# Three large and two small PSUM tiles, and softmax probabilities transposed as fp32r from a copy, in a gated encoder layer

## The chip, the cores and the metric

One NeuronCore of a Trainium2 chip runs the whole kernel. The metric is device time in microseconds (us) of one execution, as the median of repeated runs; three runs of the kernel before gave 1495.1, 1495.29 and 1495.49 us, so the time is repeatable to well under 0.1%. Beside the timed runs stands one execution under the hardware profiler, from which all durations below come.

Engines: PE is TensorE (matmul; PEld is its weight load), DVE is VectorE, ACT is ScalarE, POOL is GpSimd, SP is SyncE, which here issues the transfers.

## The reference

One layer of an encoder, applied to two groups of requests with the same weights: "prompt" with 1024 tokens and "sample" with 512, both with 1024 channels and 256 memory tokens, all in fp32.

```python
h = rms_norm(x, ln_pre)
z = h @ w_in                      # 1024 -> 6400, split into the parts below
(pool_in, pool_gate, q, k, v, attn_gate, xq, x_gate, merge_logits) = split(z)
pool_out  = multiscale_pool(pool_in, w_pool, pool_scale)        # windows 2, 4, 8, 16
q, k      = rope(rms_norm(q)), rope(rms_norm(k))                # 8 query heads, 2 key heads, 64 wide
attn_out  = softmax(q k^T / 8) v                                # over all tokens of the group
cross_out = softmax(xq mk^T / sqrt(128)) mv                     # 4 heads, 256 memory tokens
branches  = pool_out * silu(pool_gate), attn_out * silu(attn_gate), cross_out * silu(x_gate)
merged    = sum_n sigmoid(merge_logits[n] + b_merge[n]) * (branches[n] @ w_branch[n])
y         = x + rms_norm(merged @ w_out, ln_post)
```

## The kernel before, in words

**Arithmetic.** fp32 accuracy comes from fp32r matmuls in threes: each operand is split into a high part (an ACT copy into an fp32r tile, line 165) and a low part (a DVE subtraction, line 162), and `mm3` (line 132) adds high x high, high x low and low x high. Line 126 is every matmul, line 130 every transpose, so groups are told apart by their tiles. A transpose is a matmul against an identity matrix: `ident` in fp32 or `identr` in fp32r. Softmax probabilities are held in fp32 `u` tiles and transposed against `ident` into an `A` tile, from which the two parts are split.

**PSUM.** There are eight banks of 512 fp32 per partition. `A()` (line 91) is a tile of two banks, used for scores and transposes; `B()` (line 94) is a tile of one bank, used for all products. Before the change there are two A and four B tiles. SBUF tiles come from fixed sets as well: seven `u` (1024 wide), fourteen `med` (2048), eight `hu` (512).

**Stages.** The order of the work is the order of the generators at the end of the kernel (lines 1089 to 1115); a list scheduler puts the instructions of each engine in a fixed order from there, with priorities (`AHEAD`, `EVAC`, `PMAX`, `PTURN`), and each engine runs its own list strictly in order.

1. Set-up: memory keys and values (`mem_phase`), and the normalised activations of the prompt group in block form (`long_h`). The row sums of squares are spread over partitions by a matmul (`spread`, line 209) and, in `long_h`, read from the B tile by the scaling.
2. Projections of the prompt group: `products` (line 318) does pairs of weight tiles by a seven-product block scheme in place of eight. Per pair the products go to the PSUM tiles X, Y, X, Z, X, Z, X, each product being 12 matmuls of 512 columns; X keeps accumulating and is copied out in between. Behind each product `background` runs a step of the tails (rotary positions, transposes of queries and keys, pooling), which also take A and B tiles. There are 25 pairs.
3. Projections of the sample group, `plain` (line 393): 24 matmuls into one B tile for each weight tile. The first part is run alone; the second part, 32 products, is the fill of stage 4.
4. The stream: 64 units of prompt self-attention (one head, 128 queries, 1024 keys), 8 of prompt cross-attention, 16 of sample self-attention, 4 of sample cross-attention. `stream` (line 888) runs for each step i the load of unit i + 2, the scores and softmax of unit i, the transposes (`turn`) of unit i - `LAG`, and the values of unit i - `LAG` - `VLAG`. `LAG` and `VLAG` are 2. `weave` (line 108) puts fill between these parts: each part gives the fill a credit of a third of 0.66 times the unit's planned cost (2560 or 3410 ns).
5. The three gated branches of the first prompt block, run after the stream (`branches`, `merge`), then its output projection, then the other prompt block and the sample block.

**Softmax of a unit.** The scores lie in an A tile; DVE takes the maximum (line 782), ACT the exponential with its sum (line 784), DVE the reciprocal (line 785), POOL scales the probabilities (line 786). `turn` transposes the eight 128x128 pieces into another A tile, and split makes the two parts.

**Queues.** All transfers are issued on SP, in its own fixed order. Finished outputs of attention (line 886) and cross-attention (line 958) are written where they are computed, so that a write that waits for POOL or DVE holds back the loads behind it.

Of the kernel before, what the change touches and what calls it, by code (L numbers as in the profile page):

```python
# [18 lines left out]
P = 128  # L19
# [42 lines left out]
def encoder_kernel(ctx: ExitStack, tc, wt, xs, xts, mt, cols, rows, rope, edge, ys):  # L62
# [169 lines left out]
    def long_h(xt, h):  # L232

        h += [[None] * 4 for _ in range(7)]
        xv = xt.rearrange("p (k t) -> p k t", k=KC)
        q = [[M(F32) for _ in range(2)] for _ in range(2)]
        for j in range(2):
            for i in range(2):
                load(q[i][j][:].rearrange("p (c n) -> p c n", c=4), xv[:, i * 4:i * 4 + 4, j * BLK:(j + 1) * BLK])
        yield  # L240
        r, sp, sq = S(16), [], []
        for j in range(2):
            sq.append([squares(q[i][j][:]) for i in range(2)])
            yield
        for j in range(2):
            rj = r[:, j * TT:(j + 1) * TT]
            mean_squares(sq[j], rj)
            rstd_of(rj)
            yield
            sp.append(spread(rj))  # L250
            yield
        b11, b12, b21, b22 = [[q[i][j][:, :D], q[i][j][:, D:]] for i in range(2) for j in range(2)]

        def scaled(i, j):
            for c in range(4):
                x = q[i][j][:, c * BLK:(c + 1) * BLK]
                v.scalar_tensor_tensor(x, x, colt[:, i * 4 + c:i * 4 + c + 1], sp[j], op0=ALU.mult, op1=ALU.mult)
# [24 lines left out]
        put(4, t3)  # L282
        put(5, b22)
        difference(t4, b21, b11)
        put(6, t4)
# [32 lines left out]
    def products(pairs, h, n, background):  # L318
# [32 lines left out]
        for p, (_, _, take) in enumerate(pairs):  # L351
# [11 lines left out]
            for i, bank in enumerate("XYXZXZX"):  # L363
                ready(p * 4 + i // 2 + LOOK)
                start = bank not in banks
                if start:
                    banks[bank] = B()
                b = banks[bank][:, :n]
                w = ops.pop((p, i))
                for c in range(4):  # L370
                    s = slice(c * P, (c + 1) * P)
# [18 lines left out]
                next(background, None)  # L390
                yield

    def plain(pairs, h, background):

        for k0, k1, take in pairs:
            for i, key in enumerate((k0, k1)):
                w, b = weights(*key), B()
# [7 lines left out]
                yield  # L405

    def summed(b, s, out=None):

# [339 lines left out]
    def from_scratch(field, bs, dt=F32):  # L748
# [3 lines left out]
            load(t[:, c * BLK:(c + 1) * BLK], field[c][:, bs])  # L752
        return t

    def attention(b, sc, kt, vt):

        bs = slice(b * BLK, (b + 1) * BLK)
# [31 lines left out]
        def turn(i):  # L789
            jp, hd, j = units[i]  # L790
            p = state.pop(i)
            if j == 0:
                state["pt", i // 2] = M()[:], M()[:]
            pv = [t.rearrange("p (c j n) -> p c j n", c=nch, j=2) for t in state["pt", i // 2]]
            tp = A()
            for c in range(nch):
                tr(tp[:, c * P:(c + 1) * P], p[:, c * P:(c + 1) * P], ident)
            tv = tp[:].rearrange("p (c n) -> p c n", c=nch)
            with tc.high_priority(PTURN):
                split(pv[0][:, :, j], pv[1][:, :, j], tv)  # L800

# [13 lines left out]
            del state["pt", i // 2]  # L815
            gated(state, jp, hd, o, gd, out, b)

        return [(ahead, scores, turn, values, i, 2560) for i in range(len(units))]

    def pairs_of(sc, kt, vt):  # L820

# [30 lines left out]
            state[i] = p  # L852

        def turn(i):
            p, tp, pt = state[i], A(), M()
            for c in range(4):
                for j in range(2):
                    tr(tp[:, c * 256 + j * P:c * 256 + (j + 1) * P], p[:, j * BLK + c * P:j * BLK + (c + 1) * P], ident)
            with tc.high_priority(PTURN):
                split(pt[:, :D], pt[:, D:], tp[:])  # L860
            state[i] = pt

        def values(i):
# [8 lines left out]
        return [(ahead, scores, turn, values, i, 2560) for i in range(len(units))]  # L872

    def gated(state, jp, hd, o, gd, out, b):
        r = slice((hd % 2) * 64, (hd % 2) * 64 + 64)
# [7 lines left out]
            v.tensor_tensor(ot[r, :256], o[0:64, :256], ot[r, :256], op=ALU.add)  # L883
        if hd % 2:
            pool.tensor_tensor(ot[:, :256], ot[:, :256], gt[:, :256], op=ALU.mult)
            nc.sync.dma_start(out[c][:, cs], ot[:, :256])

    def stream(units):

        n = len(units)  # L890
        for i in range(-2, n + LAG + VLAG):
            more = units[min(max(i, 0), n - 1)][5] * SHARE / 3
            for k, lag in enumerate((-2, 0, LAG, LAG + VLAG)):
                if 0 <= i - lag < n:
                    units[i - lag][k](units[i - lag][4])
                if k > 0 and i >= 0:
                    yield more

    def cross(b, sc, mkd, mvd):

# [36 lines left out]

        def turn(c):
            p = state[c]
            tp = A()  # L940
            for m in range(2):
                for t in range(TT):
                    tr(tp[:, m * 512 + t * P:m * 512 + (t + 1) * P], p[:, t * 256 + m * P:t * 256 + (m + 1) * P], ident)
            pt = M()
            split(pt[:, 0:1024], pt[:, 1024:2048], tp[:])
            state[c] = pt

        def values(c):
# [9 lines left out]
            nc.sync.dma_start(out[c][:, bs], g[:])  # L958

        return [(ahead, scores, turn, values, c, 3410) for c in range(NXH)]  # L960

    def branch_parts(field, bs):
        t = from_scratch(field, bs)
# [17 lines left out]
    def merge(n, gd, bs, br, acc, merged):  # L981
# [81 lines left out]
    def ending(merged, src, dst, yv, ssq, lnpost):  # L1063
# [6 lines left out]
        for t in range(TT):  # L1070
            x = U()
            load(x, src[t * P:(t + 1) * P, :])
            o = B()[:, :256]
# [39 lines left out]
    run(block(1, 0, sc, False, merged))  # L1113
    run(block(1, 1, sc, False))
    run(block(0, 0, scs, True))
# [1 line left out]

LAG, VLAG, SHARE, LOOK, WAIT = 2, 2, 0.66, 1, 6  # L1120

AHEAD, EVAC, PMAX, PTURN, LATER = 120, 200, 150, 150, 200

# [89 lines left out]
```

## Time and profile before

| what | value |
|---|---|
| median of three runs | 1495.29 us |
| profiled execution, its own time | 1496.65 us |
| its span, first to last instruction | 1494.8 us |
| mean granted TensorE clock | 0.989 |
| busy share PE / DVE / ACT / POOL | 97 / 65 / 47 / 18% |
| share of DMA engines' time | 42.7% |

The span is 1.85 us shorter than the profiled execution's time, which is 1.36 us above the median of the runs. In the prediction, rows of a timeline have start and duration in us, engine, line, operation, output <- inputs and a count; what stands in square brackets is idle time before and what ended it. Consecutive matmuls overlap (a 512-column one is shown as 0.39 us long, but the next starts 0.23 us later), so costs of PE are read from starts. Rows of groups have the busy time, the mean in ns of one, and the idle time before them with its releasers. Wait rows have the total, the number and the longest.

### The profile page before, as it was taken

What the parts mean: (1) busy time and instruction counts of PE and PEld (TensorE: products, weight loads), DVE (VectorE), ACT (ScalarE), POOL (GpSimd) and SP (SyncE); (2) the same over time, 40 slices, a digit from 0 to 9 for tenths busy, and PEclk for the clock granted to TensorE, in tenths of its full rate; (3) what the DMA queues carried; (4) which work ended last, traced back from release to release, by engine and by line L of the source; (5) the groups of instructions that cost most, each with busy time, mean ns of one, the idle gap of its engine ahead of it and who ended that gap; (6) DMA issues with size and microseconds to landing.
All of it is one profiled execution on the core that took longest, in us unless ns stands there. A gap on an engine that the chain in (4) does not pass through costs nothing.

```text
span 1494.8 us, 19564 instructions
## 1 busy us (share of the span) xinstructions
PE 1456.0 (97%) x7264; PEld 1210.1 (81%) x7264; DVE 976.5 (65%) x1215; ACT 709.6 (47%) x1083; POOL 273.3 (18%) x286
## 2 busy tenths in 40 slices
PE   7979999999999999999999999999998999999998
PEld 5768888888888888887888888888886888888887
DVE  6996586666648564747767666676775664764764
ACT  6444444544434545434656556566675233323332
POOL 1000020110000000301222222234232150250241
PEclk9989999999999999999999999999999999999999
DMA  7513233332422434344222223165446844954952
GB/s 277 172 47 106 85 114 125 108 132 66 129 92 78 158 133 128 102 150 148 64 96 80 91 68 106 58 219 173 155 155 214 286 148 132 347 193 140 336 163 84
DMA packets 88174, 211.37 MB, mean 141 GB/s; under 512 B 9872, under 2 KB 19216, under 8 KB 87312
## 3 DMA queue, kind: packets, MB, share of 16 engines
q1 hardware_dynamic: 88080, 210.14, 42.7%
q8 instruction: 57, 0.93, 0.3%
q14 instruction: 37, 0.30, 0.1%
HBM read 155.57 MB, written 54.53 MB: 141 GB/s over the span
## 4 chain that ended last, share of the span: by engine, by line
PE 85%; DMA 4%; DVE 4%; ACT 4%; issue 2%; SPq 1%; POOL 0%; DVEq 0%; POOLq 0%; ACTq 0%
PE B L126 66%; PE A L126 14%; PE A L130 5%; ACT u L784 1%; DVE s L782 1%; ACT whi L165 1%; DMA raw<-wt 1%; DVE wlo L162 1%; PE B L130 1%; DMA hu<-xq 1%; ACT med L165 1%; SPq L139 1%; DMA u<-x_prompt 0%; DMA hu<-merge 0%; DMA hu<-x_gate 0%
## 5 line engine op out<-in xcount | busy, mean ns | idle before, releaser
L126 PE MATMUL B<-med,whi 128*128 128x512 f32 x2776 | 871.2, 394 | 15.8 <-ACT med L165 15.8
L126 PEld LDWEIGHTS B<-med,whi 128*128 128x128 f32 x2776 | 515.8, 189 | 122.2 <-ACT med L165 17.5
L126 PE MATMUL B<-med,wlo 128*128 128x512 f32 x1388 | 544.1, 392 | 0.6 <-DVE wlo L162 0.6
L126 PEld LDWEIGHTS B<-med,wlo 128*128 128x128 f32 x1388 | 261.9, 189 | 56.6 <-DVE wlo L162 1.7
L162 DVE TENSOR_TENSOR wlo<-raw,whi 128x1024 fp32r<-128x1024 f32 (+1 forms) x169 | 213.3, 1263 | 141.6 <-ACT whi L165 140.7
L165 ACT ACTIVATE whi<-raw 128x1024 fp32r<-128x1024 f32 (+1 forms) x169 | 167.5, 991 | 288.5 <-PE B L126 198.3
L165 ACT ACTIVATE med<-A 128x1024 fp32r<-128x1024 f32 x92 | 94.3, 1025 | 108.4 <-PE A L130 108.2
L162 DVE TENSOR_TENSOR med<-A,med 128x1024 fp32r<-128x1024 f32 (+1 forms) x93 | 113.0, 1215 | 42.0 <-ACT med L165 40.8
L187 POOL TENSOR_SCALAR s<-s 128x16 f32<-128x16 f32 (+3 forms) x17 | 6.9, 404 | 669.0 <-DVE s L556 333.2
L786 POOL TENSOR_SCALAR u<-u,s 128x1024 f32<-128x1024 f32 x64 | 72.1, 1127 | 251.3 <-DVE s L785 219.1
L130 PE MATMUL A<-ident,u 128*128 128x128 f32 x784 | 102.8, 273 | 0.9 <-DVE med L162 0.2
L130 PEld LDWEIGHTS A<-ident,u 128*128 128x128 f32 x784 | 90.1, 140 | 16.3 <-issue 5.2
L998 POOL TENSOR_TENSOR med<-med,hu 128x512 f32<-128x512 f32 x48 | 77.0, 1617 | 142.3 <-DVE hu L996 142.2
L782 DVE TENSOR_REDUCE s<-A 128x1 f32<-128x1024 f32 x64 | 78.1, 1220 | 32.9 <-PE A L126 11.3
L126 PE MATMUL A<-kt,med 128*128 128x512 f32 x320 | 91.9, 409 | 2.7 <-ACT u L784 1.2
L126 PE MATMUL A<-whi,med 128*128 128x512 f32 (+1 forms) x320 | 92.4, 368 | 0.2 <-ACT hu L1027 0.2
L784 ACT ACTIVATE u<-A,s 128x1024 f32<-128x1024 f32 x64 | 71.3, 1114 | 38.4 <-DVE s L782 38.0
L165 ACT ACTIVATE whi<-sum 128x1024 fp32r<-128x1024 f32 x50 | 53.1, 1062 | 65.6 <-PE B L126 63.7
L162 DVE TENSOR_TENSOR med<-med,med 128x1024 fp32r<-128x1024 f32 (+1 forms) x50 | 55.8, 1127 | 38.1 <-ACT med L165 34.2
L165 ACT ACTIVATE med<-med 128x1024 fp32r<-128x1024 f32 (+1 forms) x44 | 44.2, 1017 | 74.8 <-POOL med L998 36.2
L162 DVE TENSOR_TENSOR wlo<-sum,whi 128x1024 fp32r<-128x1024 f32 x50 | 61.1, 1221 | 23.3 <-ACT whi L165 22.4
L126 PE MATMUL B<-med,vt 128*128 128x256 f32 x512 | 75.9, 287 | 0.4 <-ACT med L165 0.4
(179 smaller groups left out, 1610.4 us busy)
## 6 DMA issues: line engine op xcount, KB each, us to landing
raw<-wt SPq DMA_DIRECT2D x168, 512.0 KB, 3.7
merge<-hu SPq DMA_DIRECT2D x72, 256.0 KB, 2.0
hu<-merge SPq DMA_DIRECT2D x72, 256.0 KB, 5.2
med<-br SPq DMA_DIRECT2D x36, 256.0 KB, 5.6
q<-hu SPq DMA_DIRECT2D x24, 256.0 KB, 2.6
br<-hu SPq DMA_DIRECT2D x24, 256.0 KB, 2.3
med<-q SPq DMA_DIRECT2D x12, 512.0 KB, 5.0
med<-xt_prompt SPq DMA_DIRECT2D x4, 1024.0 KB, 13.2
```

The costliest lines, as they stand in the source:

```text
L126: pe.matmul(out, l, r, **k)
L130: pe.transpose(out, x, i[:])
L139: return nc.sync.dma_start(out, src)
L162: v.tensor_tensor(out, x, hi.bitcast(F32), op=ALU.subtract)
L165: act.activation(hi, x, AF.Copy)
L187: pool.tensor_scalar(ss, ss, EPS, 1.0, op0=ALU.add, op1=ALU.mult)
L782: v.reduce_max(mx[:], a[:], axis=AX.X, negate=True)
L784: act.activation(p, a[:], AF.Exp, bias=mx[:], accum_out=sm[:])
L786: pool.tensor_scalar(p, p, rc[:], 1.0, op0=ALU.mult, op1=ALU.mult)
L998: pool.tensor_tensor(at, at, sg[:], op=ALU.add)
```

## The change

- A tiles go from two to three, B tiles from four to two (eight banks either way).
- In `products`, X is taken from the A tiles (half of it is used); Y and Z stay B tiles. `plain` takes its tile from a function: A and B in turn when run alone, B when it is the fill. `merge` takes A and B in turn after the stream and B within it; the last output columns take both in turn.
- In `long_h` the spread sums are copied by ACT into an `hu` tile, instead of being read in PSUM.
- Probabilities of all 92 units are copied from their `u` tile into another one declared fp32r, by a DMA of 512 KB issued on ACT (`handed`), one step after their softmax; the transposes read the copy against `identr`, into an A tile declared fp32r. `LAG` goes from 2 to 3.
- The fill is the second part of the sample projections chained with the branches of the first prompt block; in the steps behind the last unit the credit of the fill is doubled.
- Writes of finished attention outputs are collected and issued at the end of the next step.

```diff
     def A(dt=F32):
-        return ps.tile([P, 1024], dt, tag="A", bufs=2, name=nm("A"))
+        return ps.tile([P, 1024], dt, tag="A", bufs=3, name=nm("A"))
     def B(dt=F32):
-        return ps.tile([P, 512], dt, tag="B", bufs=4, name=nm("B"))
+        return ps.tile([P, 512], dt, tag="B", bufs=2, name=nm("B"))
...
-            sp.append(spread(rj))
+            sp.append(HU())
+            spread(rj, sp[j][:])
...
                 if start:
-                    banks[bank] = B()
-                b = banks[bank][:, :n]
+                    banks[bank] = (A() if bank == "X" else B())[:, :n]
+                b = banks[bank]
...
+    def either(i):
+        return (A() if i % 2 else B())[:, :BLK]
...
+    def handed(p):
+        t = U(F32R)
+        act.dma_start(t.bitcast(F32), p)
+        return t
+
+    def hand_on(state):
+        def hand(i):
+            state[i] = handed(state[i])
+        return hand
...
-            tp = A()
+            tp = A(F32R)
             for c in range(nch):
-                tr(tp[:, c * P:(c + 1) * P], p[:, c * P:(c + 1) * P], ident)
+                tr(tp[:, c * P:(c + 1) * P], p[:, c * P:(c + 1) * P], identr)
...
-            nc.sync.dma_start(out[c][:, cs], ot[:, :256])
+            finished.append((out[c][:, cs], ot[:, :256]))
...
         for i in range(-2, n + LAG + VLAG):
-            more = units[min(max(i, 0), n - 1)][5] * SHARE / 3
-            for k, lag in enumerate((-2, 0, LAG, LAG + VLAG)):
+            more = units[min(max(i, 0), n - 1)][6] * SHARE / 3 * (1 + (i >= n))
+            late = finished[:]
+            finished.clear()
+            for k, lag in enumerate((-2, 0, LAG, LAG + VLAG, 1)):
                 if 0 <= i - lag < n:
-                    units[i - lag][k](units[i - lag][4])
-                if k > 0 and i >= 0:
+                    units[i - lag][k](units[i - lag][5])
+                if 0 < k < 4 and i >= 0:
                     yield more
+            for out, x in late:
+                nc.sync.dma_start(out, x)
...
-            pj = B()
+            pj = either(d) if bare else B()
...
-    run(plain(pairs[0], hs, bg))
+    run(plain(pairs[0], hs, bg, either))
     merged = []
-    fill = drained(plain(pairs[1], hs, bg))
+    fill = drained(plain(pairs[1], hs, bg, single))
...
+    bare = False
+    fill = chain(fill, branches(0, sc, merged))
     weave(stream(units), fill)
+    bare = True
     run(fill)
-    run(branches(0, sc, merged))
...
-LAG, VLAG, SHARE, LOOK, WAIT = 2, 2, 0.66, 1, 6
+LAG, VLAG, SHARE, LOOK, WAIT = 3, 2, 0.66, 1, 6
```

More of the change, by code (lines that the diff above doesn't have):

```diff
@@ L391, in products, with plain @@
                 yield
-    def plain(pairs, h, background):
+    def plain(pairs, h, background, bank):
         for k0, k1, take in pairs:
             for i, key in enumerate((k0, k1)):
-                w, b = weights(*key), B()
+                w, b = weights(*key), bank(i)
                 for k in range(KC):
@@ L816, in values @@
             gated(state, jp, hd, o, gd, out, b)
-        return [(ahead, scores, turn, values, i, 2560) for i in range(len(units))]
+        return [(ahead, scores, turn, values, hand_on(state), i, 2560) for i in range(len(units))]
     def pairs_of(sc, kt, vt):
@@ L854, in turn @@
         def turn(i):
-            p, tp, pt = state[i], A(), M()
+            p, tp, pt = state[i], A(F32R), M()
             for c in range(4):
                 for j in range(2):
-                    tr(tp[:, c * 256 + j * P:c * 256 + (j + 1) * P], p[:, j * BLK + c * P:j * BLK + (c + 1) * P], ident)
+                    tr(tp[:, c * 256 + j * P:c * 256 + (j + 1) * P], p[:, j * BLK + c * P:j * BLK + (c + 1) * P], identr)
             with tc.high_priority(PTURN):
-                split(pt[:, :D], pt[:, D:], tp[:])
+                split(pt[:, :D], pt[:, D:], tp[:].bitcast(F32))
             state[i] = pt
@@ L870, in values @@
             gated(state, jp, hd, o, gd, out, 0)
-        return [(ahead, scores, turn, values, i, 2560) for i in range(len(units))]
+        return [(ahead, scores, turn, values, hand_on(state), i, 2560) for i in range(len(units))]
     def gated(state, jp, hd, o, gd, out, b):
@@ L939, in turn @@
             p = state[c]
-            tp = A()
+            tp = A(F32R)
             for m in range(2):
                 for t in range(TT):
-                    tr(tp[:, m * 512 + t * P:m * 512 + (t + 1) * P], p[:, t * 256 + m * P:t * 256 + (m + 1) * P], ident)
+                    tr(tp[:, m * 512 + t * P:m * 512 + (t + 1) * P], p[:, t * 256 + m * P:t * 256 + (m + 1) * P], identr)
             pt = M()
-            split(pt[:, 0:1024], pt[:, 1024:2048], tp[:])
+            split(pt[:, 0:1024], pt[:, 1024:2048], tp[:].bitcast(F32))
             state[c] = pt
@@ L957, in values @@
                 v.tensor_tensor(g[:], o[:], g[:], op=ALU.mult)
-            nc.sync.dma_start(out[c][:, bs], g[:])
-        return [(ahead, scores, turn, values, c, 3410) for c in range(NXH)]
+            finished.append((out[c][:, bs], g[:]))
+        return [(ahead, scores, turn, values, hand_on(state), c, 3410) for c in range(NXH)]
     def branch_parts(field, bs):
```

11 lines of the change are left out of this document (8 added, 3 removed).

## The prediction

> **What bounds the kernel now.** The page comes first: its span, its busy row, and the chain that ended last.
>
> ```profile
> span 1494.8 us, 19564 instructions
> ...
> PE 1456.0 (97%) x7264; PEld 1210.1 (81%) x7264; DVE 976.5 (65%) x1215; ACT 709.6 (47%) x1083; POOL 273.3 (18%) x286
> ```
>
> ```profile
> PE 85%; DMA 4%; DVE 4%; ACT 4%; issue 2%; SPq 1%; POOL 0%; DVEq 0%; POOLq 0%; ACTq 0%
> ```
>
> PE is the bound: 97% busy and 85% of the last chain. The busy share is an average, so I cut the span by stage: set-up, projections, attention and cross-attention (the "stream"), the seam behind the stream, and the branches. The columns are PE, PEld, DVE, ACT and POOL busy, then the granted clock, DMA share and GB/s.
>
> ```profile
> 50.00:100.00 50.00, 41.24 (x164) 32.52 (x164) 47.30 (x54) 23.23 (x27) 0.00 (x0) 0.86 0.34 109
> 100.00:690.00 590.00, 589.83 (x2718) 486.13 (x2716) 376.72 (x514) 261.87 (x375) 43.45 (x41) 1.00 0.35 113
> 690.00:1145.00 455.00, 449.94 (x2670) 381.81 (x2669) 312.99 (x387) 287.21 (x506) 139.77 (x168) 1.00 0.37 120
> 1145.00:1165.00 20.00, 12.91 (x45) 9.56 (x44) 7.73 (x9) 3.53 (x4) 0.00 (x0) 0.74 0.87 292
> 1165.00:1450.00 285.00, 284.36 (x1252) 234.55 (x1251) 178.17 (x179) 92.46 (x113) 80.59 (x56) 1.00 0.65 220
> ```
>
> In the projections and the branches PE hardly pauses: only less PE work could help there, and the change takes none away there. The stream is also PE-bound, 449.94 of 455 us, but it holds PE work that becomes cheaper. The seam at 1145 to 1165 has a real hole. The waits of PE say what the holes are (total, times, longest):
>
> ```profile
> PE B L126 <- ACT med L165: 16.2, 4, 7.5
> ...
> PE A L126 <- ACT u L784: 1.4, 7, 0.4
> ```
>
> The first row holds one hole of the set-up and the one of the seam. The other is scores waiting for a large PSUM tile that the softmax still reads.
>
> **Transposes, the main term.** 736 of these 784 transposes (92 units of 8; the other 48 belong to the key and query tails) turn from fp32 to fp32r. The trace already has both kinds, between the same 512-column matmuls (columns: start, busy, what).
>
> ```profile
> L130 PE MATMUL A<-ident,u 128*128 128x128 f32 x784 | 102.8, 273 | 0.9 <-DVE med L162 0.2
> ```
>
> A group of eight in fp32:
>
> ```profile
> 699.30 1.03 PE L130 MATMUL A<-ident,u 128*128 128x128 f32 x8
> 700.09 0.71 PE L126 MATMUL B<-med,whi 128*128 128x512 f32 x2
> 700.64 0.39 PE L126 MATMUL B<-med,wlo 128*128 128x512 f32 x1
> ```
>
> Four in fp32r, and eight followed by fp32 ones:
>
> ```profile
> 611.35 0.46 PE L130 MATMUL B<-identr,med 128*128 128x128 f32 x4
> 611.64 0.69 PE L126 MATMUL B<-med,whi 128*128 128x512 f32 x2
> 612.18 0.40 PE L126 MATMUL B<-med,wlo 128*128 128x512 f32 x1
> ```
>
> ```profile
> 623.90 0.80 PE L130 MATMUL B<-identr,med 128*128 128x128 f32 x8
> 624.55 1.06 PE L130 MATMUL A<-ident,med 128*128 128x128 f32 x8
> ```
>
> Busy times overlap, so starts are what counts. Eight fp32 transposes with two wide matmuls behind take 700.64 - 699.30 = 1.34 us. For fp32r, eight take 624.55 - 623.90 = 0.65 us to the next start, and the two wide ones behind a group take 612.18 - 611.64 = 0.54, together 1.19: 0.15 us less. The other way, from four fp32r (612.18 - 611.35 = 0.83) and four more at 0.65/8 = 0.081 each, gives 1.16, 0.18 less. I take 0.16 x 92 = 14.7 us, all on PE, which is the bound there; bounds 0.15 and 0.18, so 13.8 and 16.6.
>
> The Trainium skill (TensorE: Matmul & The Clock Gate, "Back-to-back issue gap") gives two figures for 128 columns, about 56 ns for matmuls alone and about 81 ns in a stream of weight load and matmul pairs; by the first, as an estimate, the term would be some 40 us. The rows' 0.65/8 = 81 ns agrees with the second, and each transpose here loads its own weights.
>
> **The seam.** The chained fill puts the first gated branch behind the last projections inside the stream, with a double share in the draining steps, and the writes of finished outputs go to SP behind the next step's loads. Today:
>
> ```profile
> 1144.21 4.37 PE L126 MATMUL B<-med,med 128*128 128x512 f32 x18
> 1155.62 2.06 PE L126 MATMUL B<-med,whi 128*128 128x512 f32 x3 [7.05 <-ACT med L165]
> ```
>
> SP's queue, and ACT behind it:
>
> ```profile
> 1145.87 0.32 SPq L958 DMA_DIRECT2D br<-hu  x1
> 1146.23 0.43 SPq L139 DMA_DIRECT2D med<-br  x1
> 1148.59 1.46 SPq L958 DMA_DIRECT2D br<-hu  x2
> 1150.10 0.43 SPq L139 DMA_DIRECT2D med<-br  x1
> ```
>
> ```profile
> 1154.51 1.06 ACT L165 ACTIVATE med<-med 128x1024 fp32r<-128x1024 f32 x1 [9.00 <-DMA med<-br]
> ```
>
> The branch's loads stand on SP between output writes that wait for PE's last values. So PE has nothing for 7.05 us, and then runs at half clock (0.74 over the window). At 0.23 us each (two wide matmuls in 700.64 - 700.09 = 0.55, with the slower first) the 45 matmuls of that window need 45 x 0.23 = 10.3 of its 20 us: 9.7 us lost. With the loads earlier and the drain interleaved I expect 8 us back; bounds 9.7 and 3. What is late next is the split of that branch's input on ACT and DVE, which needs the loads landed: the plain fill lasts as long as the stream (the planner gives it 0.66 of 2560 ns for each of 80 units and of 3410 for each of 12, 162 us; its 32 products of 24 matmuls at 512/2.4 ns are 164), so the branch starts only in the last steps and a rest of the hole may stay.
>
> **Three large tiles.** Scores and transposes rotate through three instead of two. The PE row above puts 1.4 us on the softmax; the weight-load row has more behind the same releaser:
>
> ```profile
> L126 PEld LDWEIGHTS A<-kt,med 128*128 128x128 f32 x320 | 55.5, 188 | 24.3 <-ACT u L784 10.9 <-DVE med L162 1.8 <-DMA med<-q 1.3
> ```
>
> Part of these 10.9 us is hidden under a running matmul. Bounds 1.4 and 10.9; I take 4, nearer to PE's own row.
>
> **Two small tiles.** In the stream a fill product and a unit's value sum hold one each. Evacuation against next use:
>
> ```profile
> 870.34 0.39 PE L126 MATMUL B<-med,wlo 128*128 128x512 f32 x1
> ...
> 874.22 0.63 PE L126 MATMUL B<-med,whi 128*128 128x512 f32 x2
> ```
>
> ```profile
> 871.64 0.69 ACT L479 ACTIVATE hu<-B,hbias 128x512 f32<-128x512 f32 x1
> ```
>
> A fill product ends near 870.7, is read out by 872.33, and the next one starts at 874.22, with values, scores and a transpose between: 1.9 us of cover. In the projections the sum X now lies alone in a large tile, and Y and Z have a step of X between them, 12 matmuls of 0.23 = 2.7 us, longer than that read-out. I put 1 us on it; bounds 0 and 10 (0.1 us on each of some 80 small tiles: two in each of 25 block pairs and 32 fill products). The waiting instruction would be a matmul, with all of PE behind it.
>
> **The copies.** 92 DMAs of 512 KB, SBUF to SBUF, issued on ACT; no such copy and no ACT issue is in the trace. Nearest rows:
>
> ```profile
> q1 hardware_dynamic: 88080, 210.14, 42.7%
> ...
> raw<-wt SPq DMA_DIRECT2D x168, 512.0 KB, 3.7
> ```
>
> ```profile
> 861.02 0.53 SPq L139 DMA_DIRECT2D raw<-wt  x1
> ```
>
> One unit's normalisation, and the transposes of one unit later than its own today:
>
> ```profile
> 862.37 1.12 POOL L786 TENSOR_SCALAR u<-u,s 128x1024 f32<-128x1024 f32 x1 [3.07 <-DVE s L785]
> ```
>
> ```profile
> 872.40 1.03 PE L130 MATMUL A<-ident,u 128*128 128x128 f32 x8
> ```
>
> Latency: probabilities ready at 862.37 + 1.12 = 863.49 would with a lag of three be turned at 872.40, less three savings of 0.16: 8.4 us for a copy whose like lands in 3.7. Bandwidth: 210.14 MB took 42.7% of 1494.8 us, so 0.52 MB takes 1.6 us of all engines; 92 x 1.6 = 147 us over 455 raises the stream's share from 0.37 to 0.69, and the branches run PE at 284.36 of 285 with 0.65. ACT: 287.21 us busy over 92 units is 3.1 of 4.9 us; 0.53 for the issue leaves 1.3. Queued behind a waiting issue are the exponentials and splits. So the copies are mostly covered; I take 2 us for the cross-attention end, where shares are higher; bounds 0 and 8.
>
> **Set-up.** The spread row sums go through ACT into SBUF, twice, at the price of this row:
>
> ```profile
> 32.76 0.60 ACT L221 ACTIVATE hu<-B 128x512 f32<-128x512 f32 x1 [2.08 <-PE B L126]
> ```
>
> DVE is busy 47.30 of 50 us in the stretch behind, ACT 23.23; the copies lie on ACT and DVE keeps its work. I take 0; bounds -1.5 and +2 (two copies, or the same back by an earlier free PSUM tile).
>
> **Sum:** -14.7 - 8 - 4 + 1 + 2 + 0 = -23.7 us. The profiled execution took 1496.65 us with a span of 1494.8, the median of the runs is 1495.29; the difference is taken from the median: 1471.6, say 1471.5. All good ends give -16.6 - 9.7 - 10.9 - 1.5 = -38.7 us (1456.6), all bad ones -13.8 - 3 - 1.4 + 10 + 8 + 2 = +1.8 (1497).
>
> **Rivals.** (1) *ACT becomes the bound* (slower). The copy sits in ACT's order and waits for POOL there, holding back exponentials and the read-out of large tiles. ACT has 1.3 us left per unit behind the issue; each further 0.1 us costs 9.2 us, so a wait of 1.3 + 25.7/92 = 1.6 us per copy undoes the rest of the sum (25.7 us without the 2 for copies). At 1.9 us, POOL's 1.12 and some of DVE's wait before it, it is 0.6 x 92 = 55 us: 1525. Against it: the copy is given out a whole step behind the normalisation. (2) *Small tiles run short* (slower). If every one of 80 small tiles delayed PE by 0.5 us, 40 us: 1510; it decides from 0.3 us on. For it: small tiles are halved and X leaves one bank of its tile unused. Against it: 1.9 us of cover above. The Trainium skill (Perfetto Trace Analysis, "Matmul Optimizations") asks that all eight PSUM banks be used, which speaks against the lone X; the projections' 589.83 of 590 us show slack rather than shortage. (3) *The transposes are cheaper still*: eight fp32 ones cost 1.34 less two wide matmuls, 0.88, so 0.11 each; at the 0.073 of the group of four (611.64 - 611.35 = 0.29) and with no slower matmul behind they would save 0.037 x 736 = 27 us: 1495.3 - 27 - 9 = 1459. Against it: the group of eight, and the 0.54 behind the four. (4) *The change saves only the transposes*, the seam moves to the next load and three tiles bring nothing: 1495.3 - 14.7 + 3 = 1484.
>
> **How the numbers follow.** Forecast 0.66, (4) 0.13, (1) 0.08, (2) 0.08, (3) 0.05. The range 1457 to 1488 holds the forecast's own spread and (4), and leaves out the three others. About 0.2% (3 us) is what a measurement of this kernel can tell from no change. Forecast, (3) and (4) are all faster, less a little for the bad ends: 0.83 faster, 0.04 the same, 0.13 slower.
>
> **What would show it.** Right: transposes of 92 units named identr, eight starting within 0.65 us; no PE hole over 3 us near 1120; stream about 20 us shorter; DMA share there near 0.69; PE's waits on A by the softmax gone. Wrong: PE waiting on a DMA into the copied tile, or on ACT for B tiles; ACT idle before its own DMA issues; fp32r transposes at another spacing.

## The result, and the profile after

The changed kernel took 1486.79 us (four runs, 1484.73 to 1488.2) against 1495.39 us for the kernel before: ratio 0.9939, 95% interval 0.9922 to 0.9956. That is 8.6 us or 0.6% faster, where 23.8 were forecast. The time lies inside the stated range, at its upper end, which was drawn to take in rival (4). The profiled execution took 1484.73 us, the shortest of the four, while the one before lay above its median; so the two profiled executions are 11.9 us apart, 3.3 more than the medians.

The page of the changed kernel, its span and the busy row:

```profile
span 1482.7 us, 19648 instructions
...
PE 1431.8 (97%) x7264; PEld 1197.2 (81%) x7264; DVE 967.4 (65%) x1215; ACT 710.8 (48%) x1085; POOL 273.1 (18%) x286
```

PE is busy for 24.2 us less (1456.0 before), but the span is only 12.1 us shorter: half of what was taken off PE came back as idle time. The same stages as in the prediction, from the windows of the changed kernel, show where:

```profile
100.00:690.00 590.00, 588.19 (x2707) 484.58 (x2706) 373.51 (x510) 261.27 (x374) 41.44 (x41) 1.00 0.36 114
690.00:1145.00 455.00, 431.96 (x2674) 372.22 (x2673) 307.02 (x390) 289.04 (x507) 139.44 (x168) 0.98 0.65 231
1145.00:1165.00 20.00, 20.00 (x90) 16.57 (x89) 11.03 (x13) 4.09 (x4) 0.00 (x0) 1.00 0.94 314
```

The stretch to 1145 us holds the whole stream and, since it now ends sooner, the seam too. PE is idle there for 23 us, against 5 before. The DMA share went from 0.37 to 0.65, near the 0.69 of the forecast. Who is waited for, from the waits of PE:

```profile
PE A L130 <- DMA u<-u: 17.3, 7, 7.6
...
PE A L126 <- ACT med L165: 6.7, 1, 6.7
PE B L126 <- ACT med L165: 2.5, 2, 1.3
PE A L130 <- ACT u L957: 1.5, 1, 1.5
```

The first row is new: the transposes wait 17.3 us, in seven places, for the copy of the probabilities to land. The second is the hole of the set-up, at 79 us; it was there before (7.5 us). The wait of scores for the softmax in line 784 (now 802) is gone. The row for the transposes, from the page, and that of the copies, from the part on DMA issues:

```profile
L130 PE MATMUL A<-identr,u 128*128 128x128 f32 x736 | 75.3, 246 | 19.3 <-DMA u<-u 17.3
...
u<-u ACTq DMA_DIRECT2D x92, 512.0 KB, 3.4
```

Median landing is 3.4 us, even a little less than the 3.7 that the prediction took. The answer on the tile `u` in the stream shows what a median hides (minimum, median, maximum):

```profile
L765 ACTq DMA_DIRECT2D u<-u x92: 472/472/511, 697.1 to 1128.8; - x92
...
DMA to landing us min/median/max: 2.9/3.4/9.9
```

One copy followed through the queues. SyncE gives out a burst of loads at 889 to 893 us, and the copy is issued on ScalarE in its midst. The timelines of SP, of ACT and of PE, one after the other:

```profile
889.24 0.91 SPq L139 DMA_DIRECT2D med<-q  x2
891.78 0.33 SPq L139 DMA_DIRECT2D raw<-wt  x1
892.16 0.94 SPq L139 DMA_DIRECT2D hu<-attn_gate  x1
```

```profile
890.81 0.47 ACTq L765 DMA_DIRECT2D u<-u  x1
```

```profile
895.77 1.11 PE L126 MATMUL A<-kt,med 128*128 128x512 f32 x4
899.91 1.04 PE L130 MATMUL A<-identr,u 128*128 128x128 f32 x8 [3.03 <-DMA u<-u]
```

This copy landed 9.0 us after its issue, at 899.8, and PE stood still for it from 896.9. Taken copy by copy, 16 of the 92 took over 5 us to land. From 4 us before to 3 us after the issue of one of these, SyncE gave out 4.6 transfers on average; for the other 76 it is 2.2. And the transposes start a median of 6.9 us after the issue of their copy. The Trainium skill states (DMA: Bandwidth & Descriptors, "Issuing engines are not separate DMA queues") that transfers issued by different engines run on the same 16 DMA engines and interleave; the trace agrees, as a copy issued on ScalarE beside SyncE's loads took 9.0 us here against the least of 2.9.

At the end of the stream the same happens with the last unit. The timelines of PE, SP and ACT:

```profile
1125.29 0.85 PE L130 MATMUL A<-identr,u 128*128 128x128 f32 x8 [1.51 <-ACT u L957]
1127.11 0.85 PE L130 MATMUL A<-identr,u 128*128 128x128 f32 x8 [0.96 <-DMA u<-u]
1135.60 0.85 PE L130 MATMUL A<-identr,u 128*128 128x128 f32 x5 [7.64 <-DMA u<-u]
1137.67 0.80 PE L126 MATMUL B<-med,whi 128*128 128x512 f32 x1 [1.23 <-ACT med L165]
```

```profile
1129.34 3.69 SPq L139 DMA_DIRECT2D med<-br  x4
```

```profile
1128.84 0.47 ACTq L765 DMA_DIRECT2D u<-u  x1
...
1136.56 1.06 ACT L165 ACTIVATE med<-med 128x1024 fp32r<-128x1024 f32 x1 [8.14 <-DMA med<-br]
```

The last copy goes out at 1128.84 and the four loads of the branch right behind it; the copy lands at 1135.5, the loads from 1135.9 to 1137.9. The hole that the prediction wanted to close is no shorter than before, 7.64 us against 7.05, and two things are late at once.

To split the difference, PE's time is taken between points in its order: the first scores of the stream, matmul 5448 (before the transposes of the last nine units), matmul 5811 (inside the first branch) and the last. The column "seam" thus holds the end of the stream too, and with four or five steps of lag one unit's transposes more. A gap is what the time from one start to the next exceeds the median of its kind by, where that is over 0.14 us. From the starts of all PE rows of each profiled execution, in us:

| kernel | to the first scores | stream | of it in gaps over 0.14 us | seam | rest | to last matmul |
|---|---|---|---|---|---|---|
| before | 692.4 | 410.5 | 7.8 | 74.6 | 311.1 | 1488.5 |
| changed | 691.4 | 396.9 | 13.2 | 77.3 | 310.7 | 1476.3 |

Stream -13.6, seam +2.7, set-up and projections -1.0, rest -0.4. The times from each of the 664 transposes in the stream column to the next start add up to 66.0 us before and, without one gap, to 53.7 after.

### The profile page after: what moved, and what is told of

It is laid out like the page before. It is cut to its first block, busy times and chain, and to the rows that moved or that the text cites. A ratio compares the mean times of both kernels' runs of the same rounds, so it can differ in the third digit from the quotient of the medians.

```text
span 1482.7 us, 19648 instructions
## 1 busy us (share of the span) xinstructions
PE 1431.8 (97%) x7264; PEld 1197.2 (81%) x7264; DVE 967.4 (65%) x1215; ACT 710.8 (48%) x1085; POOL 273.1 (18%) x286
## 5 line engine op out<-in xcount | busy, mean ns | idle before, releaser
L126 PE MATMUL B<-med,whi 128*128 128x512 f32 x1576 | 494.9, 394 | 4.0 <-ACT med L165 2.5
L126 PE MATMUL A<-med,whi 128*128 128x512 f32 x1200 | 374.9, 393 | 7.0 <-ACT med L165 6.7
L126 PEld LDWEIGHTS B<-med,whi 128*128 128x128 f32 x1576 | 292.8, 189 | 64.9 <-ACT med L165 3.2
L126 PE MATMUL B<-med,wlo 128*128 128x512 f32 x788 | 309.4, 393 | 0.5 <-DVE wlo L162 0.5
L126 PEld LDWEIGHTS A<-med,whi 128*128 128x128 f32 x1200 | 223.7, 188 | 54.2 <-ACT med L165 7.4
L126 PE MATMUL A<-med,wlo 128*128 128x512 f32 x600 | 234.5, 391 | 0.3 <-DVE wlo L162 0.3
L126 PEld LDWEIGHTS B<-med,wlo 128*128 128x128 f32 x788 | 148.5, 188 | 32.6 <-DVE wlo L162 1.4
L126 PEld LDWEIGHTS A<-med,wlo 128*128 128x128 f32 x600 | 112.9, 188 | 24.7 <-DVE wlo L162 0.9
L804 POOL TENSOR_SCALAR u<-u,s 128x1024 f32<-128x1024 f32 x64 | 72.1, 1126 | 219.5 <-DVE s L803 179.0
L130 PEld LDWEIGHTS A<-identr,u 128*128 128x128 f32 x736 | 72.4, 141 | 33.3 <-issue 14.6
L130 PE MATMUL A<-identr,u 128*128 128x128 f32 x736 | 75.3, 246 | 19.3 <-DMA u<-u 17.3
```

What stands on the lines that cost most here:

```text
L126: pe.matmul(out, l, r, **k)
L130: pe.transpose(out, x, i[:])
L804: pool.tensor_scalar(p, p, rc[:], 1.0, op0=ALU.mult, op1=ALU.mult)
```

## The experiments

Theory after the result: the copies are the loss. A copy that is given out in a burst of loads lands after the transposes want it, in the stream and at its end. Rivals: the fp32r transposes save less than the rows said; the tiles lose what they gain; the copies cost through what they take from other transfers or from ScalarE. Each row is against the kernel before on the same chip (1493.84 to 1495.39 us); rows of different chips are best compared by the last column. In these later runs the kernel before took 1492.95 to 1497.51 us, so it repeats to 0.3% and not to 0.1%.

| run | median us | ratio, 95% interval | less than before, us |
|---|---|---|---|
| the change | 1486.79 | 0.9939 (0.9922 to 0.9956) | 8.6 |
| no copies, fp32r tile written by GpSimd | 1466.16 | 0.9813 (0.9797 to 0.9829) | 28.7 |
| transposes and copies alone | 1495.34 | 0.9999 (0.999 to 1.0008) | -0.5 |
| tiles alone | 1486.37 | 0.9942 (0.993 to 0.9955) | 8.5 |
| chained fill alone | 1494.03 | 0.9997 (0.9988 to 1.0005) | 0.9 |
| change, share 0.72 | 1484.51 | 0.994 (0.9928 to 0.9953) | 9.5 |
| change, last four units direct | 1481.76 | 0.9917 (0.9903 to 0.993) | 12.2 |
| change, both of these | 1481.01 | 0.9916 (0.9903 to 0.993) | 13.0 |
| change, LAG 4 | 1477.06 | 0.989 (0.9875 to 0.9905) | 16.9 |
| change, LAG 4, last four direct | 1468.59 | 0.9833 (0.9818 to 0.9847) | 25.3 |
| change, LAG 5, last four direct | 1475.29 | 0.9872 (0.9859 to 0.9886) | 18.6 |
| change, transposes undone | 1487.3 | 0.9946 (0.9933 to 0.996) | 6.5 |
| the same with unread copies | 1488.05 | 0.9957 (0.9944 to 0.9969) | 5.8 |

### No copies

```diff
-            pool.tensor_scalar(p, p, rc[:], 1.0, op0=ALU.mult, op1=ALU.mult)
-            state[i] = p
+            t = U(F32R)
+            pool.tensor_scalar(t, p, rc[:], 1.0, op0=ALU.mult, op1=ALU.mult)
+            state[i] = t
...
-            state[i] = handed(state[i])
+            pass
```

> The changed kernel, but POOL writes the scaled probabilities straight into an fp32r tile and no copy is made (this rounds the probabilities to fp32r before they are split, so their low part is lost). Theory, late copies: the fp32r transposes did save their 14.5 us, and the 92 copies gave some 10 us of it back in the stream, where seven transposes wait for a copy that landed late behind a burst of loads, and some more at the seam. Then without them the time is 1471 to 1475 us. Rival, small tiles: the loss is the two B tiles and the ACT queue, and the copies are innocent; then it stays at 1485 to 1488.

1466.16 us, 20 us under the change and below the theory's range. As its probabilities lose their low part, this kernel is only there to tell what the copies cost. Its waits of PE have no row for `DMA u<-u` any more. The longest wait of the first row below is at the seam; the second row is the set-up's:

```profile
PE B L126 <- ACT med L165: 7.2, 2, 5.9
PE A L126 <- ACT med L165: 6.7, 1, 6.7
```

In the terms of the first table its stream is 386.0 us, 10.9 less than with the copies, its seam 73.0, 4.3 less, and its last matmul 13.7 us earlier. The medians differ by more, because the profiled execution is the longest of this kernel's four (1471.09 us at a granted clock of 0.988; another took 1465.23 at 0.993) and the shortest of the change's. So the copies as built cost 14 us by the profiles and 20 by the medians, not 2; the profiles do not show where the other 6 us go. The 5.9 us at the seam are the branch's loads; they remain when the copies are gone.

### Each part alone on the kernel before

For the transposes: the functions `handed` and `hand_on`, the fp32r tiles and identity, and `LAG` 3, with two large and four small tiles and the old fill.

```diff
-            tp = A()
+            tp = A(F32R)
...
-LAG, VLAG, SHARE, LOOK, WAIT = 2, 2, 0.66, 1, 6
+LAG, VLAG, SHARE, LOOK, WAIT = 3, 2, 0.66, 1, 6
```

> The kernel before with the copies, the fp32r transposes and the lag of three alone; two large and four small tiles, no chained fill. Theory, late copies: 14.5 us saved, 10 lost to late copies and up to 5 at the end of the stream, where the last unit's copy lengthens the chain: 1490 to 1496 us. Rival, small tiles: with four small tiles the saving shows in full, 1482 us or less.

1495.34 us, no difference. Its transposes start as closely as in the change (53.6 us for 658 of them without one gap), and the gaps in the stream rise from 7.8 to 19.5 us. From its waits of PE:

```profile
PE A L130 <- DMA u<-u: 6.3, 5, 2.2
PE A L130 <- issue: 3.3, 2, 1.7
PE A L126 <- ACT u L795: 3.2, 4, 1.9
PE B L126 <- DVE med L162: 3.1, 3, 1.6
```

What the transposes save comes back as waits, 6.3 us of it for the copy itself. That the other rows are work held up behind a late copy was not shown.

For the tiles: all of the tile edits and the spread sums copied into SBUF.

```diff
-        return ps.tile([P, 1024], dt, tag="A", bufs=2, name=nm("A"))
+        return ps.tile([P, 1024], dt, tag="A", bufs=3, name=nm("A"))
...
-        return ps.tile([P, 512], dt, tag="B", bufs=4, name=nm("B"))
+        return ps.tile([P, 512], dt, tag="B", bufs=2, name=nm("B"))
```

> The kernel before with three large and two small tiles alone (X in a large one, the spread sums copied to SBUF, products alone taking both kinds in turn). Theory: waits of scores on a large tile go, 6 to 11 us saved, 1484 to 1489 us. Rival, small tiles: PE waits for them in the fill and the projections, 1495 us or more.

1486.37 us: the tiles alone give as much as the whole change. Stream 404.7 us (5.8 less), seam 72.1 (2.5 less); the gaps over 0.14 us in the stream hardly move (7.4), so the gain lies in waits shorter than that at each tile. The weight loads of the scores show them: the idle time before these, of which 10.9 us out of 24.3 were put down to the softmax in line 784, is down to 10.6, and that releaser is gone:

```profile
L126 PEld LDWEIGHTS A<-kt,med 128*128 128x128 f32 x320 | 56.3, 188 | 10.6 <-DMA med<-q 1.5
```

The small tiles do cost something in the projections. From matmul 2500 to 2800 every traced kernel with the tile edits takes 63.4 us, every one without them 61.6. Of these 1.8 us, 1.3 are one wait for a small tile that ScalarE is still reading out (line 421); in the changed kernel:

```profile
617.02 0.74 PE L126 MATMUL B<-med,whi 128*128 128x512 f32 x2 [1.31 <-ACT med L421]
```

For the chained fill, with the doubled credit and the later writes:

```diff
+    fill = chain(fill, branches(0, sc, merged))
     weave(stream(units), fill)
     run(fill)
-    run(branches(0, sc, merged))
```

> The kernel before with the chained fill, the doubled credit at the end and the late writes alone. Theory, the last copy: it is the last unit's copy that kept the seam open, so without copies the hole of 7 us and the clock's dip go, 5 to 9 us saved, 1486 to 1490 us. Rival, late loads: the branch's loads land no earlier because they are given out as late as before, so the hole stays: 1493 to 1496 us.

1494.03 us: the hole stays. The timelines of its PE and its SP:

```profile
1138.57 1.91 PE L130 MATMUL A<-ident,u 128*128 128x128 f32 x16
1147.10 0.80 PE L126 MATMUL B<-med,whi 128*128 128x512 f32 x1 [6.62 <-ACT med L165]
```

```profile
1139.54 0.42 SPq L139 DMA_DIRECT2D hu<-merge  x1
1140.24 0.32 SPq L480 DMA_DIRECT2D merge<-hu  x1
1140.61 1.98 SPq L139 DMA_DIRECT2D med<-br  x4
```

The writes no longer stand between the loads (the four `med<-br` go out together), but the loads are given out when the generator of the branch reaches them, and it reaches them when the projections are used up: at 1140.6, when PE's last transposes of the stream are done too (1140.5).

### The seam in the changed kernel

The share of the fill from 0.66 to 0.72, so that the branch begins some units earlier:

```diff
-LAG, VLAG, SHARE, LOOK, WAIT = 3, 2, 0.66, 1, 6
+LAG, VLAG, SHARE, LOOK, WAIT = 3, 2, 0.72, 1, 6
```

> The changed kernel with the fill's share raised from 0.66 to 0.72 and nothing else, so that the side's last projections are used up some 50 us earlier and the branch's products run between the last units. Theory (the seam's hole comes from the branch's loads, given out only when the fill reaches them; those start at 1129 us of the changed kernel): the loads go out well before the last unit, the 7.64 us and 1.23 us waits at the seam shrink to what the last unit's copy alone costs, and the run comes out 3 to 8 us under the changed kernel, 1478 to 1484. Rival (the last unit's own chain of copy, transposes and split is the later of the two): the hole moves by under 2 us and the time stays at 1485 to 1488. Second rival: the fill runs out in the last units, which then lose 5 to 10 us in bare waits, 1488 to 1496.

1484.51 us, just above the theory's range and inside the interval of the change. The first loads of the branch go out at 1105 us instead of 1129, the wait for the last copy is gone, but there are holes elsewhere: for a copy given out beside those loads, and at the seam, now at 1156, for the next loads of the branch, given out at 1155. Its timeline of PE:

```profile
1109.80 0.84 PE L130 MATMUL A<-identr,u 128*128 128x128 f32 x8 [2.74 <-DMA u<-u]
...
1162.78 2.05 PE L126 MATMUL B<-med,whi 128*128 128x512 f32 x3 [6.31 <-ACT med L165]
```

The last four units transposed straight from their fp32 tile:

```diff
-        return [(ahead, scores, turn, values, hand_on(state), c, 3410) for c in range(NXH)]
+        return [(ahead, scores, turn, values, hand_on(state) if copied else lambda c: None, c, 3410) for c in range(NXH)]
...
-    units += pairs_of(scs, kts, vts) + cross(0, scs, mkd[0], mvd[0])
+    units += pairs_of(scs, kts, vts) + cross(0, scs, mkd[0], mvd[0], False)
```

> The changed kernel with the stream's last four units transposed from the first tile in fp32, with no copy; all else stays. Theory (loads are late at the seam): the wait for the copied tile there goes, a wait of 6 to 9 us for the branch's operand stays in the same place, and the time is 1485 to 1488. Rival (the last unit's copy is the later one): the seam closes to about 2 us and the time falls to 1479 to 1483.

1481.76 us, 4 to 5 less than the change, the time that the rival had, though the seam keeps 5 us of waits and not 2. Its timeline of PE at the seam:

```profile
1131.57 0.76 PE L130 MATMUL A<-ident,u 128*128 128x128 f32 x5 [1.39 <-POOL u L961]
1135.89 0.80 PE L126 MATMUL B<-med,whi 128*128 128x512 f32 x1 [3.56 <-ACT med L165]
```

So my theory of the seam (the loads alone) was wrong: the last copy's chain held PE the longer of the two (7.64 us against 1.23), and without it the loads leave 3.56 us. The seam column is 72.5 us, 4.8 less than in the change.

> Both edits of the last two at once. If either late thing suffices for the hole, only this run closes it: 1476 to 1481, while each edit alone stays at 1484 to 1488. If the loads alone were the cause, this run equals the one with the larger share within 2 us. If the copy alone, it equals the one with the last four units transposed directly.

Both edits at once: 1481.01 us, the same as the direct end within its interval. The earlier loads add nothing here.

### More time for the copies

```diff
-LAG, VLAG, SHARE, LOOK, WAIT = 3, 2, 0.66, 1, 6
+LAG, VLAG, SHARE, LOOK, WAIT = 4, 2, 0.66, 1, 6
```

> The changed kernel with the transposes four steps behind their scores in place of three, so that each copy has one step (some 6.4 us) more to land. Theory (the copies cost time because those given out in a burst of loads land in 6 to 9 us, later than the transposes want them): the waits for the copied tile inside the stream, 9.7 us in the profile of the changed kernel without the seam's, go to under 2 us, and the time falls by 5 to 12 us to 1475 to 1482, less if the longer drain at the end takes 2 to 4 us of it back. Rival (the copies cost time by what they take from other transfers and from the issuing engine): the time stays at 1484 to 1489. Second rival: one more live tile for a unit's rows makes the row pool the bound, and the scores wait: over 1490.

1477.06 us, some 8 less than the change, in the theory's range. The landing is what it was (answer on the tile `u` in the stream):

```profile
DMA to landing us min/median/max: 2.9/3.4/8.5
```

But the transposes now want a copy 11.3 us after its issue (6.9 before), and every copy but the last three has landed at least 1.7 us ahead of them. The waits of PE and its timeline at the seam:

```profile
PE A L130 <- DMA u<-u: 10.4, 2, 8.9
```

```profile
1121.69 1.23 PE L130 MATMUL A<-identr,u 128*128 128x128 f32 x8 [8.93 <-DMA u<-u]
1124.39 0.34 PE L130 MATMUL A<-identr,u 128*128 128x128 f32 x1 [1.47 <-DMA u<-u]
```

All that is left of the wait for copies is at the seam; ahead of it, it went from six places to none. Stream 388.7 us, gaps 3.4.

The two edits that helped, together:

> The two edits that each helped, together: transposes four steps behind their scores, and the last four units transposed from the first tile in fp32 without a copy. With four steps the seam's hole grew to 8.9 us of waiting for the copied tile, at the branch's loads. Theory (late copies are the loss, in the stream and at the seam, and the two add): the wait at the seam falls to the 3 to 5 us that the branch's own loads leave, and the time is 1469 to 1474, 4 to 8 us under the run with four steps alone. Rival (the branch's loads are as late as the last copy once the stream ends sooner): 1475 to 1478, no gain over four steps alone.

1468.59 us: some 17 less than the change and 25.3 less than the kernel before. The two largest rows of its waits of PE (17.1 us together) lie before 80 us, in the set-up. Then come:

```profile
PE B L126 <- ACT med L165: 4.4, 2, 3.1
PE A L130 <- DVE med L162: 1.7, 1, 1.7
```

There is no row for `DMA u<-u`; 3.07 us of the first row are the branch's loads at the seam. Stream 390.5 us and seam 67.3. Its window over the stream, and the same window of the changed kernel:

```profile
690.00:1100.00 410.00, 406.36 (x2526) 350.96 (x2525) 288.42 (x368) 270.18 (x467) 130.90 (x153) 1.00 0.66 234
```

```profile
690.00:1100.00 410.00, 398.30 (x2464) 342.71 (x2463) 282.66 (x358) 261.93 (x447) 126.14 (x147) 1.00 0.64 228
```

PE's idle time falls from 11.7 to 3.6 us with no less DMA, and 62 more matmuls get into the stretch.

One step more, with the direct end:

> As the last, with five steps in place of four. Theory (with four steps every copy inside the stream has landed 5 us or more before its transposes): nothing is left to gain, the time is within 2 us of the run with four steps and the direct end, or 1 to 3 us more for one more step of drain. Rival (the copies still delay the stream at four steps): another 2 to 4 us less. Second rival: seven row tiles don't hold one more live step, and the scores wait: 1480 or more.

1475.29 us, 6.7 more than with four steps; both numbers of the theory were too low. Its premise was off as well: with four steps the least margin of a copy was 1.7 us, not 5. No copy is waited for here either, and stream and seam are those of four steps within 0.7 us (391.2 and 67.9). The loss is behind the seam: the rest takes 316.9 us against 310.9. Its timeline shows one wait there for the branch's next operand,

```profile
1154.83 0.50 PE L126 MATMUL B<-med,whi 128*128 128x512 f32 x1 [2.70 <-ACT med L165]
```

with matmuls at double spacing behind it until 1159.4. The wait, and half of the 3.4 us at half clock, are some 4.4 of the 6 us. What put that load later was not tried and stays open.

### The transposes undone, and copies that nothing reads

```diff
-            tp = A(F32R)
+            tp = A()
...
-            state[i] = handed(state[i])
+            pass
...
-LAG, VLAG, SHARE, LOOK, WAIT = 3, 2, 0.66, 1, 6
+LAG, VLAG, SHARE, LOOK, WAIT = 2, 2, 0.66, 1, 6
```

> The changed kernel with its transposes and copies undone: fp32 transposes straight from the first tile, two steps behind the scores, no copies; tiles, companions, chained fill, doubled credit and late writes stay. Theory (tiles give 8.5 us, the chain about 1, and they add): 1484 to 1487, the same as the changed kernel within 2 us, so that the transposes' own part is worth nothing as built. Rival (tiles and chain help each other): 1478 to 1483, and then the copied transposes as built cost more than they save.

1487.3 us, the same as the change. As built, transposes and copies together are worth nothing that can be measured (the intervals overlap), and tiles and chain do not help each other.

```diff
-            pass
+            handed(state[i])
```

> The last kernel with the 92 copies still issued, into tiles that nothing reads: it makes copies for nothing, and its transposes read the first tile. What it is slower by than the one without copies is what the copies cost by themselves (issue on ScalarE, transfers beside the loads, row tiles), with no engine waiting for their landing. Theory (the copies' cost is the wait for their landing): within 2.5 us of the kernel without copies. Rival (the copies cost by what they take from the loads, 46 MB each way in 430 us): 5 to 12 us slower than it.

1488.05 us, 0.75 more. The windows over the stream of this kernel and of the one without copies:

```profile
690.00:1100.00 410.00, 406.74 (x2447) 352.09 (x2446) 278.86 (x355) 259.44 (x443) 128.65 (x145) 1.00 0.62 223
```

```profile
690.00:1100.00 410.00, 405.61 (x2435) 351.42 (x2434) 283.40 (x353) 262.76 (x443) 125.06 (x143) 1.00 0.36 115
```

Nearly the same PE work, 0.62 against 0.36 of DMA: the 92 copies cost nothing that can be told from the spread of the runs (some 2 us) as transfers and as issues on ScalarE. Their cost is the wait for their landing: it is gone when nothing waits for them, and most of it when they get a step more and the last four units do without.

## Why the prediction was wrong

The direction and the bound (PE) were right. The sum was -23.7 us and 8.6 came; two terms failed, and one was too small. With the sizes below (transposes -14.7, tiles -8.5, chained fill -0.9, copies +14 to +20) the sum is -10 to -4, and the -8.6 measured lies within.

- **Copies: +2 forecast, 14 to 20 measured. This is the step that failed.** The step said that a copy has 8.4 us and "like lands in 3.7". The 8.4 counted from the end of GpSimd's scaling. The copy is a step of the generator and goes out a median of 1.9 us behind that, and the transposes start 6.9 us after it. And 3.7 was a median of loads; 16 of 92 copies took 5 to 9.9 us. A median landing says nothing about a wait that ends on the slowest. The trace of before showed the spread in part. In its stream the loads `raw<-wt`, of the same 512 KB, land within 6.4 us, which the 6.9 would have covered; in its branches, at the DMA share of 0.65 that the copies bring to the stream, they take up to 8.8 (the rows of the tile `raw` from 690 to 1145 us and from 1165 to 1450):

```profile
DMA to landing us min/median/max: 3.5/3.7/6.4
DMA to landing us min/median/max: 3.3/4.1/8.8
```

The bound of 8 us was too low for the same reason. The bandwidth half of the step was right (0.65 against 0.69 forecast, and the unread copies cost 0.75 us), as was the room on ScalarE.
- **Seam: -8 forecast, +2.7 in the profile and -0.9 alone.** The step knew that the branch starts only in the last steps, and that "a rest of the hole may stay". Nearly all of it stayed: the loads are issued when the fill reaches the branch. And the last unit's copy, a serial step that the change adds to the end of the stream, wasn't in the term at all. With that copy gone and four steps of room the seam column falls by 7.3 us. That does not bear out the 8: the tiles alone take 2.5 us off that column, and cheaper transposes of the stream's last units lie in it too.
- **Three large tiles with two small ones: -3 forecast, -8.5 measured.** I took PE's own row (1.4 us) as the nearer end; the weight-load row (10.9 us) was the nearer one. The +1 for small tiles in it was about right, 1.8 us in the projections.
- **Transposes: -14.7 forecast, and right.** The starts of 664 of the 736 in the stream fall by 12.3 us, so 13.6 for all; two wide matmuls behind a group take 0.535 us in place of 0.547, 1.1 more for 92. The kernel without copies and the one without the transposes' part differ by 16.4 us in the stream column, 13.7 of it starts of transposes.
- **Set-up: 0 forecast**, and no size can be read: PE's hole there ends at 79.5 us with the change and 81.3 before, but at 80.2 and 81.5 in two kernels (the chain and the copies alone) that leave the set-up as it was.
- **Rivals.** (1) and (2) did not come: ScalarE has no wait before its DMA issues that shows in PE's time (the unread copies), and small tiles cost the 1.8 us above, not 40. (3) did not: the spacing is that of the group of eight. (4), the transposes alone with the seam left open, has nearly the time that came, 1484, but for the wrong reason: the tiles gave what it denied them, and the copies took what it granted. That "PE waiting on a DMA into the copied tile" would show the forecast wrong was on its list.

With four steps and a direct end, so with most of the copies' wait taken away, the kernel gains 25.3 us, near the sum that was forecast. That is in part luck: the tiles gave 8.5 us where the sum had 3, and the seam less than its 8. What remains between that kernel and the one without copies is 2.4 to 3.4 us; it was not taken apart.

## What to carry to other kernels

A transfer put into a dependent chain is priced by its slowest landing beside the bursts of loads that share its DMA engines, and from its issue, not from the moment its input is ready; if the slack is less than that, add a step of lag before giving up on it. Two late things can hold up the same place, so take each away, alone and together, before judging either. At the end of a pipelined loop an added step has little left to hide behind (the last copy held PE for 7.6 us): there the dearer operation without the extra step can be the better one.

## What the runs showed of the hardware

A copy of 512 KB from SBUF to SBUF lands in 2.9 us at the least and in up to 9.9 us beside a burst of loads, while its issue takes ScalarE 0.47 to 0.51 us. The Trainium skill (SBUF — State Buffer, "The DMA setup-cost knee") gives about 2 us plus the bytes at 436 GB/s, by which such a copy is an estimate of 3.2 us; the trace's median of 3.4 agrees, and the 16 slow ones lie outside it. 48 MB more through the DMA engines within some 430 us, at 0.62 of their time, made 0.75 us of difference where nothing waited for them, which is inside the intervals.

A short wait can cost more than its length. After the 3.03 us at 899.91 PE ran at half clock until about 903.4, and at the seam from its restart until 1142.7; matmuls of 512 columns start 0.43 us apart there and 0.23 us afterwards. It is not so after every wait: the one of 2.80 us at 976.56 in the same trace was followed by none of it. The windows of the changed kernel, with the granted clock as the third number from the end:

```profile
899.90:903.40 3.50, 3.49 (x14) 2.95 (x15) 1.29 (x2) 2.12 (x3) 0.00 (x0) 0.55 0.37 150
1135.60:1142.70 7.10, 5.87 (x22) 4.95 (x23) 3.57 (x4) 3.52 (x4) 1.18 (x1) 0.51 0.62 245
976.00:984.00 8.00, 7.44 (x56) 6.93 (x57) 3.87 (x6) 5.38 (x12) 1.12 (x1) 1.00 0.72 279
```
